# A hybrid decoder layer on one core: first loads in halves, key norms first, and a float32 block as three float32r products with the subtract on GpSimd

## The chip, the core and the metric

The kernel is one launch on one core of a Trainium2 chip. The metric is the device time of the launch in microseconds, from the first to the last instruction and what lies around it. Engines are named as in the profile: PE (TensorE matmuls), PEld (its weight loads), DVE (VectorE), ACT (ScalarE), POOL (GpSimd), SP (SyncE, which issues most transfers).

## What is computed

One layer over 256 tokens of width 2048, all in float32:

```python
h = _rmsnorm(x, ln1_g)
q, k, v, u = split(h @ w_in)             # 1024 | 256 | 256 | 1024 columns
q = _rmsnorm(q per head, q_norm_g); k = _rmsnorm(k per head, k_norm_g)
y_attn = _sliding_window_attention(q, k, v, attn_sinks, rel_bias)   # window 128
y_ssm = _s5_mixer(u, ...)                # 64 groups of 16 channels, 64 complex states, GELU, GLU
mixed = concat(_rmsnorm(y_attn, attn_out_g), _rmsnorm(y_ssm, ssm_out_g))
x = x + mixed @ w_out
h2 = _rmsnorm(x, ln2_g)
out = x + (silu(h2 @ w_ff_gate) * (h2 @ w_ff_up)) @ w_ff_down
```

Only the first part matters here: the projection to u (two blocks of 512 columns, `w_u`), the S5 mixer that feeds on u, the projection to q, k and v (three blocks of 512, `w_qkv`), and the norms of keys and queries.

## The kernel before

**Products.** A projection goes in blocks of 512 output columns. For both token tiles (t = 0, 1; 128 tokens each) a block sums 16 products of 128 rows of the weights. Weights come in pieces of two such row groups (`KD = 2`, 512 KB, tile `w`, four buffers), loaded by SP in the order of use (`Weights.fetch`, L436).

Most blocks run through `block` (L497): each factor is split in a high part that float32r holds exactly and a low part, and three float32r products stand for the float32 one: high x high (L513), high x low weight (L514), low x high weight (L515). `Weights._piece` splits a piece: ACT casts the high part (`whi`, L462), DVE subtracts it from the piece (`wlo`, L463). Both have two buffers (`split`), so that a cast waits until PE is done with the piece two before. A piece is 2 row groups x 2 token tiles x 3 = 12 products.

The two blocks of u run through `block32` (L522) instead: plain float32 products of `xt` (x transposed, scaled by the norm's weights) and the unsplit pieces, L530. The trace shows two passes for each such product. `xt` is four tiles that share memory with `sm` and `qn`, hence their names in the rows. `hT` and `lT` are the high and low part of `xt` (`split_x`, L605 and L606), which the w_qkv blocks use.

**S5.** The scan over 256 tokens is turned into small matrices: `tables` makes powers of the state's factor from a chain of small DVE and ACT steps; `matrices(q, h)` makes, for a quarter q of the channel groups and a half h of it, `cm` (L242, L243) and `bm` (L249, L250) on DVE from those tables and the coefficients, 128x1024 elements a step; PE multiplies and transposes them (`pk` L254, `pt_bm` L264). `tokens(q)` fetches u again from DRAM (`ut`, issued on POOL's queue, L283), where ACT's queue has put it (`ud`, L645); `states` and `outputs` do the scan and its outputs (`px`, `pa`, `pb`, `zz`, `hh`, `py`). The products of tokens within a chunk need a matrix `mt` that POOL's queue moves by way of DRAM (`kd` L272, `mt` L276).

**Order.** The program is written with priorities (`prio`) and a scheduler sets a fixed order for every engine. What POOL's or DVE's next instruction waits for holds up all behind it. The S5 steps (`STEPS`, priority 20,000) are spread among the matmuls of the u blocks (30,000 and 32,000) and the w_qkv blocks (60,000). The coefficients of quarters 2 and 3 are loaded into the memory of `xt` once that is free.

**Norms of keys and queries** (L703 to L728, priority 65,000). For each token tile: squares of its keys (ACT, L713), sums per head (DVE, L715), mean and epsilon (L716), the power -0.5 on POOL (L717, 128x4); the same for the queries (128x16); a scaling of the queries' factors (L718); the keys' scaling (L721). Then the keys are transposed on PE (`pt_k`, L725).

**Start.** SP issues the constants (`pack`, L391), then by turns a quarter of `xT` and a piece of `w_u`; ACT squares the quarter, DVE scales it in place (L601).

Of the kernel before, what the change touches and what calls it, by code (L numbers as in the profile page):

```python
# [10 lines left out]
F32 = mybir.dt.float32  # L11
F32R = mybir.dt.float32r
AF = mybir.ActivationFunctionType
ALU = mybir.AluOpType
AX = mybir.AxisListType
# [3 lines left out]
P = 128  # L19
D = 2048  # L20
L = 256
NT = L // P
HD = 64
NH = 16
NKV = 4
# [9 lines left out]
EPS = 1e-6  # L35
NEG = -1e30
NB = 512
KD = 2
# [21 lines left out]
def dap(t, dims, off=0):  # L60
    return bass.AP(t.tensor, t.offset + off, [list(d) for d in dims])


def bc(ap, pos, n):
    dims = [list(d) for d in ap.ap]
    dims.insert(pos, [0, n])
    return bass.AP(ap.tensor, ap.offset, dims)
# [319 lines left out]
def consts(tc, nc, cp, ins):  # L387

    c = {}
    pack = cp.tile([P, sum(n for _, n in COLS)], F32, name="pack")  # L390
    nc.sync.dma_start(pack, ins["c_pack"])  # L391
    at = 0
    for name, n in COLS:
        c[name] = pack[:, at : at + n]
        at += n
    c["halfpi"] = cp.tile([P, 1], F32, name="halfpi")
    nc.vector.memset(c["halfpi"], math.pi / 2)
    c["mhalf"] = cp.tile([P, NH + NKV], F32, name="mhalf")
    nc.vector.memset(c["mhalf"], -0.5)
    c["ones"] = cp.tile([P, 32], F32, name="ones")  # L400
    nc.vector.memset(c["ones"], 1.0)
    c["v32"] = cp.tile([P, 2], F32, name="v32")
    nc.vector.memset(c["v32"], 1.0 / 32)
    return c
# [20 lines left out]
class Weights:  # L425
# [5 lines left out]
        self.place = -100_000  # L431
        self.marks = []

    def fetch(self, src):
        w = self.raw.tile([P, KD, NB], F32, name="w", tag="w")
        self.nc.sync.dma_start(w, src)  # L436
        self.ready.append(w)

    def whole(self, src):
# [6 lines left out]
        self.marks.append([None])  # L446
        return [w[:, i] for i in range(KD)]

    def piece(self, src):
        was, self.tc.cur_priority = self.tc.cur_priority, self.place  # L450
        out = self._piece(src)
        self.place, self.tc.cur_priority = self.tc.cur_priority, was
        return out

    def _piece(self, src):
        nc = self.nc
        if not self.ready:
            self.fetch(src)
        w = self.ready.pop(0)
        hi = self.split.tile([P, KD, NB], F32R, name="whi", tag="whi")  # L460
        lo = self.split.tile([P, KD, NB], F32R, name="wlo", tag="wlo")
        self.marks.append([nc.scalar.copy(hi, w).ins])  # L462
        nc.vector.tensor_tensor(lo, w, hi.bitcast(F32), op=ALU.subtract)  # L463
        return [(hi[:, i], lo[:, i]) for i in range(KD)]


# [1 line left out]
def layer_kernel(ctx: ExitStack, tc: tile.TileContext, ins, out):  # L468
    nc = tc.nc
    v, s, pe = nc.vector, nc.scalar, nc.tensor  # L470
# [7 lines left out]
    wts = Weights(tc, nc, raw, split)  # L478

    @contextmanager  # L480
    def prio(at):

        was, tc.cur_priority = tc.cur_priority, at
        try:
            yield
        finally:
            tc.cur_priority = was
# [6 lines left out]
        nc.gpsimd.tensor_tensor(r, t, cst["mhalf"][:, :cols], op=ALU.pow)  # L494
        return r

    def block(hi, lo, wsrc, k0=0, behind=None, apart=False):  # L497


        acc = [ps.tile([P, NB], F32, name=f"acc{t}", tag="mm") for t in range(NT)]  # L500
        nk = KD * len(wsrc)
        k = 0
        for n, src in enumerate(wsrc):
            parts = wts.piece(src)
            turns = [(i, t) for i in range(KD) for t in range(NT)]
            if apart and n == len(wsrc) - 1:
                turns.sort(key=lambda it: it[1])
            for i, t in turns:
                whi, wlo = parts[i]
                xh = hi[:, k0 + k + i, t * P : (t + 1) * P]  # L510
                xl = lo[:, k0 + k + i, t * P : (t + 1) * P]
                first, last = k + i == 0, k + i == nk - 1
                mm = pe.matmul(acc[t], lhsT=xh, rhs=whi, start=first, stop=False)  # L513
                pe.matmul(acc[t], lhsT=xh, rhs=wlo, start=False, stop=False)  # L514
                pe.matmul(acc[t], lhsT=xl, rhs=whi, start=False, stop=last)  # L515
            k += KD
            wts.marks[-1].append(mm.ins)
            if behind and n in behind:
                behind[n](mm.ins)
        return acc  # L520

    def block32(x, wsrc):  # L522

        acc = [ps.tile([P, NB], F32, name=f"acc{t}", tag="mm") for t in range(NT)]
        nk = KD * len(wsrc)
        k = 0
        for src in wsrc:
            for w in wts.whole(src):
                for t in range(NT):
                    mm = pe.matmul(acc[t], lhsT=x(k)[:, t * P : (t + 1) * P], rhs=w, start=k == 0, stop=k == nk - 1)  # L530
                k += 1
            wts.marks[-1].append(mm.ins)
        return acc

    def pieces(w, nb, kg0, kgs):
        return [w[nb, kg] for kg in range(kg0, kg0 + kgs)]
# [33 lines left out]
    qn = [rt.tile([P, AW], F32, name=f"qn{t}") for t in range(NT)]  # L570
    kvn = [rt.tile([P, 2 * NKV * HD], F32, name=f"kvn{t}") for t in range(NT)]
# [4 lines left out]
    hT = stat.tile([P, D // P, L], F32R, name="hT", tag="shi")  # L576
    lT = stat.tile([P, D // P, L], F32R, name="lT", tag="slo")
    xt = [(sm + qn)[i].rearrange("p (k l) -> p k l", l=L) for i in range(4)]
    with prio(-300_000):
        cst = consts(tc, nc, cpool, ins)  # L580
        ident, g1 = cst["ident"], cst["g1"]
        ssm = Ssm(tc, nc, sp, ps, dpool, ins, cst)
        first = pieces(ins["w_u"], 0, 0, 4)
        for k4 in range(4):
            nc.sync.dma_start(xt[k4], ins["xT"][:, 4 * k4 : 4 * k4 + 4])
            wts.fetch(first[k4])
            if k4 == 0:
                ssm.load()
        ssm.coefficients(0, nc.sync)
    with prio(-99_990):  # L590
# [12 lines left out]
    def split_x(k4):  # L603
        ks = slice(4 * k4, 4 * k4 + 4)
        s.copy(hT[:, ks], xt[k4])  # L605
        v.tensor_tensor(lT[:, ks], xt[k4], hT[:, ks].bitcast(F32), op=ALU.subtract)  # L606
# [28 lines left out]
        nc.gpsimd.dma_start(td, mk)  # L635


    ngc = G // GC
    for nb in range(SW // NB):
        with prio(30_000 + 2_000 * nb):  # L640
            acc = block32(lambda k: xt[k // 4][:, k % 4], pieces(ins["w_u"], nb, 0, 16 // KD))
            for t in range(NT):
                un = kvn[t] if nb else sp.tile([P, NB], F32, name="un", tag="hh", bufs=2)
                s.activation(un, acc[t], AF.Copy, scale=r1[:, t : t + 1])
                nc.scalar.dma_start(ssm.ud[nb * (NB // UB) : (nb + 1) * (NB // UB), t * P : (t + 1) * P]  # L645
                                    .rearrange("b p x -> p b x"), un.rearrange("p (b x) -> p b x", x=UB))
    with prio(20_100):
        for k4 in range(4):
            split_x(k4)
        for q in range(2, ngc):  # L650
            ssm.coefficients(q, nc.sync, sm[q - 2])
    with prio(60_000):
# [47 lines left out]


    kT = at.tile([P, NKV // 2, 2, L], F32, name="kT")
    rq = []  # L703
    with prio(65_000):
        nc.gpsimd.memset(kT, 0.0)
        sk = at.tile([P, NH], F32, name="sk")
        nc.gpsimd.dma_start(sk, dap(ins["attn_sinks"], [[0, P], [1, NH]]))
        for t in range(NT):
            sh = at.tile([P, NH + NKV], F32, name=f"sh{t}")
            r_ = at.tile([P, NH + NKV], F32, name=f"rqk{t}")  # L710
            for src, o, n in ((kvn[t][:, : NKV * HD], NH, NKV), (qn[t], 0, NH)):
                sq = at.tile([P, n * HD], F32, name="sq", tag="lg", bufs=2)
                s.activation(sq, src, AF.Square)  # L713
                part = sh[:, o : o + n]
                v.tensor_reduce(part, sq.rearrange("p (h d) -> p h d", d=HD), axis=AX.X, op=ALU.add)  # L715
                v.tensor_scalar(part, part, 1.0 / HD, EPS, op0=ALU.mult, op1=ALU.add)  # L716
                nc.gpsimd.tensor_tensor(r_[:, o : o + n], part, cst["mhalf"][:, :n], op=ALU.pow)  # L717
            v.tensor_scalar_mul(r_[:, :NH], r_[:, :NH], HD**-0.5)  # L718
            rq.append(r_)
            kk = kvn[t][:, : NKV * HD].rearrange("p (h d) -> p h d", d=HD)  # L720
            v.tensor_tensor(kk, kk, bc(r_[:, NH:], 2, HD), op=ALU.mult)  # L721
        pt = ps.tile([P, 2, L], F32, name="pt_k", **WORK)
        for i in range(2):
            for t in range(NT):
                pe.transpose(pt[:, i, t * P : (t + 1) * P], kvn[t][:, i * P : (i + 1) * P], ident)  # L725
        for a in range(2):
            ks = slice(a * HD, (a + 1) * HD)
            s.activation(kT[ks, :, a], pt[ks], AF.Copy, scale=cst["qkg"][ks, 1:2])  # L728
# [67 lines left out]
    with prio(70_000):  # L796
        lg = [weights(0)]
# [166 lines left out]
```

## Time and profile before

| | us |
|---|---|
| median of 3 runs | 1066.72 (1064.7 to 1066.95) |
| the profiled execution | 1064.85 |
| its span, first to last instruction | 1063.1 |
| PE busy | 1043.2 (98%) |
| PEld busy | 820.8 (77%) |
| DVE busy | 610.9 (57%) |
| ACT busy | 485.4 (46%) |
| POOL busy | 56.1 (5%) |

The granted clock of PE is 0.999 of full speed over the span. A busy PE is not PE at its peak: products overlap in the pipeline, and their ends are modelled. What one costs is read from start to start. Shares over the whole span mix stages: the two u blocks and the w_qkv blocks lie in the first 175 us, the long feed-forward stage behind them is another matter.

### The profile page before, as it was taken

The page shows a single profiled execution, that of the slowest core. Times are in us where ns is not written, and L with a number is a line of the kernel's source. Part 1 is how long each engine was busy: PE and PEld are TensorE (multiplying, and loading weights), DVE is VectorE, ACT ScalarE, POOL GpSimd, SP SyncE. Part 2 cuts the span into 40 slices and gives each one's busy share as a digit, 9 for nine tenths or more (in the row PEclk, how much of TensorE's full clock was granted, in tenths as well). Part 3 has the DMA queues.
Part 4 walks back from the last instruction along what each step waited for, and adds up shares of the span by engine and source line. Part 5 has one row for each costly group of instructions (what it writes and reads, how often), then busy time and mean ns, then how long its engine had stood idle before and what let it go on. Part 6 is the DMA issues. An engine that isn't in the chain of part 4 may idle for free.

```text
span 1063.1 us, 13209 instructions
## 1 busy us (share of the span) xinstructions
PE 1043.2 (98%) x5048; PEld 820.8 (77%) x5048; DVE 610.9 (57%) x755; ACT 485.4 (46%) x665; POOL 56.1 (5%) x87
## 2 busy tenths in 40 slices
PE   7999988999999999999999999999999999999998
PEld 3457776767788888888888888888888888888886
DVE  6988975788556454445554455545555444444443
ACT  5244556665445444444444444444444333333332
POOL 2030325000000000000000000000000000000000
PEclk9999999999999999999999999999999999999999
DMA  7677567434455556555555555555655556565653
GB/s 268 191 197 237 152 180 267 165 109 139 158 189 167 182 193 189 189 183 194 189 189 195 180 197 185 193 191 184 198 181 196 179 190 207 195 201 195 203 192 101
DMA packets 62015, 199.08 MB, mean 187 GB/s; under 512 B 11328, under 2 KB 14000, under 8 KB 61632
## 3 DMA queue, kind: packets, MB, share of 16 engines
q1 hardware_dynamic: 52800, 184.89, 53.3%
q0 software_dynamic: 3264, 9.29, 3.3%
q10 hardware_dynamic: 5888, 4.06, 1.3%
q8 instruction: 39, 0.64, 0.3%
q14 instruction: 24, 0.20, 0.1%
HBM read 193.47 MB, written 4.74 MB: 186 GB/s over the span
## 4 chain that ended last, share of the span: by engine, by line
PE 85%; DVE 8%; ACT 2%; DMA 2%; issue 2%; POOL 1%; SPq 0%; DVEq 0%; POOLq 0%; ACTq 0%
PE acc L514 26%; PE acc L515 26%; PE acc L513 26%; PE acc L530 2%; DVE wlo L463 1%; PE pt_f L872 1%; DMA zd<-za 1%; POOL rqk L717 1%; PE po L786 1%; DVE bm L249 1%; ACT whi L462 1%; DVE cm L242 1%; DVE bm L250 1%; DVE tm L249 1%; DVE cm L243 1%
## 5 line engine op out<-in xcount | busy, mean ns | idle before, releaser
L463 DVE TENSOR_TENSOR wlo<-w,whi 128x1024 fp32r<-128x1024 f32 x328 | 401.7, 1225 | 407.4 <-ACT whi L462 407.1
L462 ACT CAST whi<-w 128x1024 fp32r<-128x1024 f32 x328 | 345.1, 1052 | 473.1 <-PE acc L515 461.4
L513 PE MATMUL acc<-whi,pTh 128*128 128x512 f32 x704 | 275.0, 391 | 0.0
L514 PE MATMUL acc<-wlo,pTh 128*128 128x512 f32 x704 | 274.0, 389 | 0.2 <-DVE wlo L463 0.2
L515 PE MATMUL acc<-whi,pTl 128*128 128x512 f32 x704 | 274.1, 390 | 0.1
L515 PEld LDWEIGHTS acc<-whi,pTl 128*128 128x128 f32 x704 | 132.1, 188 | 28.0 <-DVE pTl L564 0.5
L514 PEld LDWEIGHTS acc<-wlo,pTh 128*128 128x128 f32 x704 | 132.2, 188 | 27.6 <-DVE wlo L463 0.7
L513 PEld LDWEIGHTS acc<-whi,pTh 128*128 128x128 f32 x704 | 132.2, 188 | 27.6 <-ACT pTh L563 0.5
L513 PE MATMUL acc<-whi,fhi 128*128 128x512 f32 x352 | 139.0, 395 | 0.0
L514 PE MATMUL acc<-wlo,fhi 128*128 128x512 f32 x352 | 138.9, 395 | 0.0
L515 PE MATMUL acc<-whi,flo 128*128 128x512 f32 x352 | 138.9, 394 | 0.0
L515 PEld LDWEIGHTS acc<-whi,flo 128*128 128x128 f32 x352 | 66.3, 188 | 15.5
L513 PEld LDWEIGHTS acc<-whi,fhi 128*128 128x128 f32 x352 | 66.3, 188 | 15.5
L514 PEld LDWEIGHTS acc<-wlo,fhi 128*128 128x128 f32 x352 | 66.3, 188 | 15.3
L513 PE MATMUL acc<-whi,mT 128*128 128x512 f32 x128 | 50.9, 397 | 0.8 <-ACT mT L563 0.8
L514 PE MATMUL acc<-wlo,mT 128*128 128x512 f32 x128 | 50.5, 394 | 0.0
L515 PE MATMUL acc<-whi,nT 128*128 128x512 f32 x128 | 50.3, 394 | 0.0
L514 PE MATMUL acc<-wlo,hT 128*128 128x512 f32 x96 | 38.6, 402 | 2.8 <-DVE wlo L463 2.8
L515 PE MATMUL acc<-whi,lT 128*128 128x512 f32 x96 | 38.0, 396 | 0.0
L513 PE MATMUL acc<-whi,hT 128*128 128x512 f32 x96 | 37.7, 398 | 0.0
L530 PE MATMUL acc<-w,sm 128*128 128x512 f32 x64 | 30.7, 628 | 6.7 <-DVE sm L601 6.7
L884 ACT ACTIVATE sl<-acc,r 128x256 f32<-128x256 f32 x44 | 20.8, 472 | 20.7 <-PE acc L515 20.7
(258 smaller groups left out, 822.0 us busy)
## 6 DMA issues: line engine op xcount, KB each, us to landing
w<-in_w_gu SPq DMA_DIRECT2D x176, 512.0 KB, 3.3
w<-in_w_down SPq DMA_DIRECT2D x88, 512.0 KB, 3.4
w<-in_w_out SPq DMA_DIRECT2D x32, 512.0 KB, 3.3
w<-in_w_qkv SPq DMA_DIRECT2D x24, 512.0 KB, 4.3
w<-in_w_u SPq DMA_DIRECT2D x16, 512.0 KB, 4.0
w<-in_w_glu SPq DMA_DIRECT2D x8, 512.0 KB, 4.3
bias<-td POOLq DMA_DIRECT2D x4, 512.0 KB, 5.1
x<-in_x POOLq DMA_DIRECT2D x2, 1024.0 KB, 10.4
```

Source lines behind the costliest of these rows:

```text
L242: v.tensor_tensor(dst, bc(c[:, i, hs], 2, T), bc(e, 3, GP), op=ALU.mult)
L243: v.tensor_tensor(cmh[:, :, 1:], cmh[:, :, 1:], tm, op=ALU.subtract)
L249: v.tensor_tensor(dst, bc(b[:, i, hs], 2, T), bc(e, 3, GP), op=ALU.mult)
L250: v.tensor_tensor(bm2, bm2, tm2, op=ALU.add)
L462: self.marks.append([nc.scalar.copy(hi, w).ins])
L463: nc.vector.tensor_tensor(lo, w, hi.bitcast(F32), op=ALU.subtract)
L513: mm = pe.matmul(acc[t], lhsT=xh, rhs=whi, start=first, stop=False)
L514: pe.matmul(acc[t], lhsT=xh, rhs=wlo, start=False, stop=False)
L515: pe.matmul(acc[t], lhsT=xl, rhs=whi, start=False, stop=last)
L530: mm = pe.matmul(acc[t], lhsT=x(k)[:, t * P : (t + 1) * P], rhs=w, start=k == 0, stop=k == nk - 1)
L717: nc.gpsimd.tensor_tensor(r_[:, o : o + n], part, cst["mhalf"][:, :n], op=ALU.pow)
L884: s.activation(sl, acc[t][:, :256], AF.Silu, scale=r2[:, t : t + 1])
```

## The change

- The constants are loaded on ACT's queue. The first quarter of `xT` and the first piece of `w_u` come in halves, the first half of `xT` first. The small S5 inputs (`ssm.load`) are issued after the second quarter and piece.
- The second block of u runs through `block` with `hT` and `lT`: three float32r products, eight pieces cast on ACT, and their low parts subtracted on POOL (`rest=nc.gpsimd`). The split of `xt` is written ahead of the u blocks.
- The norms: keys of both token tiles first, with their scaling, then the queries of both.

```diff
-    nc.sync.dma_start(pack, ins["c_pack"])
+    nc.scalar.dma_start(pack, ins["c_pack"])
...
-    def fetch(self, src):
+    def fetch(self, src, parts=1):
         w = self.raw.tile([P, KD, NB], F32, name="w", tag="w")
-        self.nc.sync.dma_start(w, src)
+        n = KD // parts
+        for i in range(0, KD, n):
+            self.nc.sync.dma_start(w[:, i : i + n], src[:, i : i + n])
...
-        nc.vector.tensor_tensor(lo, w, hi.bitcast(F32), op=ALU.subtract)
+        rest.tensor_tensor(lo, w, hi.bitcast(F32), op=ALU.subtract)
...
         for k4 in range(4):
-            nc.sync.dma_start(xt[k4], ins["xT"][:, 4 * k4 : 4 * k4 + 4])
-            wts.fetch(first[k4])
             if k4 == 0:
+                nc.sync.dma_start(xt[0][:, :2], ins["xT"][:, :2])
+                wts.fetch(first[0], KD)
+                nc.sync.dma_start(xt[0][:, 2:], ins["xT"][:, 2:4])
+            else:
+                nc.sync.dma_start(xt[k4], ins["xT"][:, 4 * k4 : 4 * k4 + 4])
+            if k4:
+                wts.fetch(first[k4])
+            if k4 == 1:
                 ssm.load()
...
+    with prio(20_100):
+        for k4 in range(4):
+            split_x(k4)
     ngc = G // GC
     for nb in range(SW // NB):
         with prio(30_000 + 2_000 * nb):
-            acc = block32(lambda k: xt[k // 4][:, k % 4], pieces(ins["w_u"], nb, 0, 16 // KD))
+            src = pieces(ins["w_u"], nb, 0, 16 // KD)
+            if nb == 0:
+                acc = block32(lambda k: xt[k // 4][:, k % 4], src)
+            else:
+                acc = block(hT, lT, src, rest=nc.gpsimd)
...
+        def head_norms(t, src, o, n):
+            sq = at.tile([P, n * HD], F32, name="sq", tag="lg", bufs=2)
+            s.activation(sq, src, AF.Square)
+            part = sh[t][:, o : o + n]
+            v.tensor_reduce(part, sq.rearrange("p (h d) -> p h d", d=HD), axis=AX.X, op=ALU.add)
+            v.tensor_scalar(part, part, 1.0 / HD, EPS, op0=ALU.mult, op1=ALU.add)
+            nc.gpsimd.tensor_tensor(rq[t][:, o : o + n], part, cst["mhalf"][:, :n], op=ALU.pow)
+
+        for t in range(NT):
+            head_norms(t, kvn[t][:, : NKV * HD], NH, NKV)
+        for t in range(NT):
             kk = kvn[t][:, : NKV * HD].rearrange("p (h d) -> p h d", d=HD)
-            v.tensor_tensor(kk, kk, bc(r_[:, NH:], 2, HD), op=ALU.mult)
+            v.tensor_tensor(kk, kk, bc(rq[t][:, NH:], 2, HD), op=ALU.mult)
+        for t in range(NT):
+            head_norms(t, qn[t], 0, NH)
+            v.tensor_scalar_mul(rq[t][:, :NH], rq[t][:, :NH], HD**-0.5)
```

How the order moves at three places. POOL, behind the mask for the bias (`td`), before: transfers of u (`ut`) and of the S5 matrix (`kd`, `mt`):

```order
L494 TENSOR_TENSOR r_275<-r_a,mhalf 128x2
L635 DMA td<-mk 16x384
L283 DMA ut<-ud 128x512 x2
L272 DMA kd_107<-kt_105 128x1x64 x4
L276 DMA mt_111<-kd_107 16x256
```

and in the change, the low parts of the second u block (L465) among them:

```order
L643 DMA td<-mk 16x384
L465 TENSOR_TENSOR wlo<-w,whi 128x1024 x2
L283 DMA ut<-ud 128x512
L465 TENSOR_TENSOR wlo<-w,whi 128x1024 x2
L283 DMA ut<-ud 128x512
L465 TENSOR_TENSOR wlo<-w,whi 128x1024
L272 DMA kd_112<-kt_110 128x1x64 x3
L465 TENSOR_TENSOR wlo<-w,whi 128x1024
L272 DMA kd_112<-kt_110 128x1x64
L465 TENSOR_TENSOR wlo<-w,whi 128x1024
```

From the third on the subtracts stand behind transfers that have waits of their own; the eighth follows behind four of the `mt` transfers.

PE, from the end of the first u block (`acc_289`) into the second, before, where `pk` is the first half group's product of S5 matrices:

```order
L530 MATMUL acc_289<-w,qn_76 128x512
L530 MATMUL acc_336<-w,sm_79 128x512
L254 MATMUL pk<-cm,bm_853 32x128 x8
L264 MATMUL pt_bm<-pack,bm_853 128x128 x8
L530 MATMUL acc_337<-w,sm_79 128x512
```

and in the change, where eleven float32r products of the second block stand ahead of that group (the last two here):

```order
L515 MATMUL acc_347<-whi,hT 128x512
L516 MATMUL acc_347<-wlo,hT 128x512
L254 MATMUL pk<-cm,bm_951 32x128 x8
L264 MATMUL pt_bm<-pack,bm_951 128x128 x8
L517 MATMUL acc_347<-whi,lT 128x512
```

The groups of S5 keep their order on PE; the number of products between them changes. From the seventh half group on they stand at the same or nearly the same product of the w_qkv blocks as before.

ACT at the S5 tables, before (`qs` belongs to the sum of squares of x, `cm` to the first matrices, L162 is the last sine):

```order
L159 ACTIVATE wa<-wa 128x64
L547 COPY qs<-pq 128x256
L238 ACTIVATE cm<-sc,sign 128x8x16 x2
L605 CAST hT<-qn_76 128x1024
L160 ACT_TABLE_LOAD
L160 ACTIVATE wa<-wa 128x64
L161 ACTIVATE wa<-wa 128x64
L162 ACTIVATE wa<-wa,halfpi 128x64
```

and in the change:

```order
L613 CAST hT<-qn_76 128x1024
L549 COPY qs<-pq 128x256
L238 ACTIVATE cm<-sc,sign 128x8x16
L160 ACT_TABLE_LOAD
L160 ACTIVATE wa<-wa 128x64
L161 ACTIVATE wa<-wa 128x64
L238 ACTIVATE cm<-sc,sign 128x8x16
L162 ACTIVATE wa<-wa,halfpi 128x64
```

The copy and the two `cm` steps, which stood ahead of the last cast, now stand behind it.

## Rows read from the trace of the kernel before

**Rows 1.** busy time by windows: us, PE, PEld, DVE, ACT, POOL (instructions), PEclk, DMA share, GB/s

```profile
20.00:124.00 104.00, 103.13 (x630) 63.73 (x628) 95.73 (x145) 45.42 (x76) 23.11 (x44) 1.00 0.70 199
...
330.00:1063.10 733.10, 728.67 (x3231) 599.33 (x3229) 358.17 (x339) 305.26 (x329) 0.69 (x1) 1.00 0.58 188
```

**Rows 2.** waits of PE, 0 to 320 us: in total, times, longest

```profile
PE acc L514 <- DVE wlo L463: 3.5, 5, 2.2
```

**Rows 3.** timeline at the seventh half group: start us, us, engine, line, instruction [idle before it]

```profile
122.37 1.23 DVE L250 TENSOR_TENSOR bm<-bm,tm 128x1024 f32<-128x1024 f32 x1
...
124.11 0.64 PE L254 MATMUL pk<-cm,bm 128*32 128x128 f32 x16
```

**Rows 4.** timeline of PE: passes of float32 products, then float32r products

```profile
65.22 10.03 PE L530 MATMUL acc<-w,qn 128*128 128x512 f32 x23
...
146.17 0.39 PE L514 MATMUL acc<-wlo,hT 128*128 128x512 f32 x1
...
148.89 0.39 PE L514 MATMUL acc<-wlo,hT 128*128 128x512 f32 x1
```

**Rows 5.** groups by line: count | busy us, mean ns | idle before

```profile
L462 ACT CAST whi<-w 128x1024 fp32r<-128x1024 f32 x328 | 345.1, 1052 | 473.1 <-PE acc L515 461.4
...
L243 DVE TENSOR_TENSOR cm<-cm,tm 128x1024 f32<-128x1024 f32 x7 | 8.5, 1218 | 0.0
...
L705 POOL MEMSET kT<- 128x1024 f32 x1 | 1.0, 972 | 0.0
```

**Rows 6.** timeline of DVE and POOL, 178 to 187 us

```profile
178.52 3.92 POOL L717 TENSOR_TENSOR rqk<-sh,mhalf 128x16 f32<-128x16 f32 x2 [3.49 <-DVE sh L716]
...
178.63 1.23 DVE L463 TENSOR_TENSOR wlo<-w,whi 128x1024 fp32r<-128x1024 f32 x1
...
181.48 0.17 DVE L718 TENSOR_SCALAR rqk<-rqk 128x16 f32<-128x16 f32 x1 [0.50 <-POOL rqk L717]
...
182.89 1.22 DVE L463 TENSOR_TENSOR wlo<-w,whi 128x1024 fp32r<-128x1024 f32 x1
...
183.06 3.81 POOL L717 TENSOR_TENSOR rqk<-sh,mhalf 128x16 f32<-128x16 f32 x1 [0.62 <-DVE sh L716]
```

**Rows 7.** timeline of ACT and DVE at the S5 tables

```profile
17.43 0.37 ACT L547 COPY qs<-pq 128x256 f32<-128x256 f32 x1 [0.61 <-PE pq L544]
...
17.70 0.69 ACT L238 ACTIVATE cm<-sc,sign 128x128 f32<-128x128 f32 x2
...
20.45 0.54 DVE L633 TENSOR_TENSOR mk<-pb,mk 16x384 f32<-16x384 f32 x1
...
21.45 0.23 DVE L165 SCALAR_TENSOR_TENSOR wa<-wa 128x64 f32<-128x64 f32 x1
```

**Rows 8.** timeline of the first loads

```profile
0.75 0.39 SPq L391 DMA_DIRECT2D pack<-in_c_pack  x1
...
2.96 0.43 DVE L207 TENSOR_TENSOR dg<-pack 128x256 f32<-128x256 f32 x1 [1.65 <-DMA pack<-in_c_pack]
...
5.33 1.34 ACT L612 ACTIVATE sq<-sm 128x256 f32<-128x256 f32 x4 [3.09 <-DMA sm<-in_xT]
...
5.78 1.27 DVE L601 TENSOR_SCALAR sm<-sm,pack 128x256 f32<-128x256 f32 x4 [2.40 <-ACT sq L612]
...
6.75 8.09 PE L530 MATMUL acc<-w,sm 128*128 128x512 f32 x14 [6.75 <-DVE sm L601]
```

**Rows 9.** timeline of PE and DVE at the key and query norms

```profile
182.95 0.55 PE L725 MATMUL pt_k<-pack,kvn 128*128 128x128 f32 x3 [1.37 <-DVE kvn L721]
...
186.90 0.17 DVE L718 TENSOR_SCALAR rqk<-rqk 128x16 f32<-128x16 f32 x1 [2.79 <-POOL rqk L717]
```

**Rows 10.** waits of DVE, 20 to 124 us: in total, times, longest

```profile
DVE wlo L463 <- ACT whi L462: 5.1, 4, 1.7
```

**Rows 11.** timeline of ACT's and POOL's queues at u

```profile
42.85 0.37 ACTq L645 DMA_DIRECT2D ud<-un  x1
...
46.60 0.57 POOL L283 DMA_DIRECT2D ut<-ud  x1 [24.77 <-DMA ud<-un]
```

More of the change, by code (lines that the diff above doesn't have):

```diff
@@ L447, in whole, with piece, _piece @@
         return [w[:, i] for i in range(KD)]
-    def piece(self, src):
+    def piece(self, src, rest=None):
         was, self.tc.cur_priority = self.tc.cur_priority, self.place
-        out = self._piece(src)
+        out = self._piece(src, rest or self.nc.vector)
         self.place, self.tc.cur_priority = self.tc.cur_priority, was
         return out
-    def _piece(self, src):
+    def _piece(self, src, rest):
         nc = self.nc
@@ L495, in rsqrt_mean, with block @@
         return r
-    def block(hi, lo, wsrc, k0=0, behind=None, apart=False):
+    def block(hi, lo, wsrc, k0=0, behind=None, apart=False, rest=None):
         acc = [ps.tile([P, NB], F32, name=f"acc{t}", tag="mm") for t in range(NT)]
@@ L503, in block @@
         for n, src in enumerate(wsrc):
-            parts = wts.piece(src)
+            parts = wts.piece(src, rest)
             turns = [(i, t) for i in range(KD) for t in range(NT)]
@@ L647, in layer_kernel @@
     with prio(20_100):
-        for k4 in range(4):
-            split_x(k4)
         for q in range(2, ngc):
@@ L702, in layer_kernel @@
     kT = at.tile([P, NKV // 2, 2, L], F32, name="kT")
-    rq = []
     with prio(65_000):
@@ L707, in layer_kernel @@
         nc.gpsimd.dma_start(sk, dap(ins["attn_sinks"], [[0, P], [1, NH]]))
-        for t in range(NT):
[L709 to L719, printed above, removed]
+        sh = [at.tile([P, NH + NKV], F32, name=f"sh{t}") for t in range(NT)]
+        rq = [at.tile([P, NH + NKV], F32, name=f"rqk{t}") for t in range(NT)]
+        def head_norms(t, src, o, n):
[5 more added lines that the diff above has]
+            nc.gpsimd.tensor_tensor(rq[t][:, o : o + n], part, cst["mhalf"][:, :n], op=ALU.pow)
+        for t in range(NT):
+            head_norms(t, kvn[t][:, : NKV * HD], NH, NKV)
+        for t in range(NT):
             kk = kvn[t][:, : NKV * HD].rearrange("p (h d) -> p h d", d=HD)
-            v.tensor_tensor(kk, kk, bc(r_[:, NH:], 2, HD), op=ALU.mult)
+            v.tensor_tensor(kk, kk, bc(rq[t][:, NH:], 2, HD), op=ALU.mult)
+        for t in range(NT):
+            head_norms(t, qn[t], 0, NH)
+            v.tensor_scalar_mul(rq[t][:, :NH], rq[t][:, :NH], HD**-0.5)
         pt = ps.tile([P, 2, L], F32, name="pt_k", **WORK)
```

## The prediction

> **What bounds the kernel now.** I read the table of windows first. In the last 733.1 us PE is busy for 728.7 [rows 1]: nothing there is touched, so whatever PE gains or loses before 330 us is the change in the time. In the stretch from 20 to 124 us two engines are full at once: PE 103.13 of 104.00 us, DVE 95.73, which leaves DVE 8.3 us of idle time. POOL has 23.1 us of work there [rows 1]. So the question is not only how much PE work goes, but whether DVE can follow.
>
> Next the waits of PE up to 320 us: the largest behind the start is 3.5 us in all, for low parts of weights [rows 2]. So PE sets the pace, with few holes. How close DVE is behind shows at the seventh half group of S5 matrices: its last DVE step (L250) starts at 122.37 and takes 1.23, its first matmul on PE runs at 124.11 [rows 3]. That place, half a microsecond after DVE, is my yardstick: when does PE pass it in the change? In both orders the same DVE instructions and 150 products of the w_qkv blocks stand ahead of it.
>
> **The change part by part.** *Second column block of u.* It ran as 32 float32 products of two passes each; 23 passes take 10.03 us, so a pass 0.43 [rows 4] and the block 64 x 0.43 = 27.5 us. It becomes 96 float32r products; from 146.17 to 148.89 there are twelve, 0.227 each [rows 4], so 21.8 us. PE saves 5.7 us. It needs eight more casts of 1.05 us on ACT [rows 5] and eight subtracts. ACT is 45 us busy of 104 in the stretch [rows 1], and a piece on PE lasts 12 x 0.227 = 2.7 us, so the casts cost nothing while they follow each other in time; without that cover each is 1.05.
>
> *The subtract on GpSimd.* No subtract of 128x1024 runs on POOL in this trace. From below: POOL writes 128x1024 in 0.97 us [rows 5], one stream. From above: two reads and one write one after the other at that rate, 2.9. On DVE the same operation takes 1.23 [rows 6]. I take two streams, 1.94 us, since a read and a write can overlap but the two reads are the extra: 15.5 us for eight. POOL has the time. The question is what it does to DVE, whose steps in this stretch are nearly all tensor_tensors with two operands in SBUF (L243 is one of four such lines, 1.22 us each [rows 5]), as the subtract is.
>
> For that the trace has one telling pair. The power of 128x16 on POOL begins at 178.52 and has released DVE at 181.48, 2.9 us; the next one, the same shape, begins at 183.06 and takes 3.81 [rows 6]. The difference of 0.9 us fits the subtract that DVE had begun at 182.89, which ran 1.05 us into it [rows 6]. POOL seems to have stood until DVE was done. In the other direction DVE began a subtract 0.11 us after POOL began its power and took 1.23 as always [rows 6]; but the power reads only 16 elements per partition, at its start, so that says little of an operation that reads 1024.
>
> The Trainium skill, SBUF — State Buffer, "Who interferes with whom", says that a DVE instruction with two SBUF inputs and a GpSimd instruction that reads SBUF exclude each other, and that whichever comes second is blocked for the whole of the first. The longer power agrees with it; the DVE subtract at 178.63, unhindered for the 2.9 us of the first power, does not, so the "whole instruction" is not what this trace shows. GPSIMD Engine Reference, "Elementwise — side-by-side cycle accounting", gives 4497 ns for a float32 tensor_tensor of 2048 elements; an estimate from that figure is 2.25 us per subtract, and the sum below would be 1075.9 instead of 1073.4. No run here shows it.
>
> So I take it that subtract and DVE step go one after the other, whichever comes first. Then DVE's and POOL's work adds up: at the yardstick DVE needs 124.1 - 8.3 (all its idle time used) + 15.5 + 1.3 = 132.6 us. The 1.3 is a later start of the S5 tables: in the new ACT order the copy qs and one cm row stand between the last cast and the table load, and another cm row ahead of the last sine (L162), three steps of some 0.27 from start to start, 0.8 us, and DVE waits for that sine with L165; and the 0.54 us of L633, which lay in DVE's wait, now stands behind the tables [rows 7].
>
> *First loads.* Transfers are issued from 0.75; the constants (122 KB) land 2.2 us after their issue, the first 512 KB of x at 5.33, and PE begins at 6.75 [rows 8]. With the constants on ACT's queue, the first half of x goes out at 0.75 and needs 256 KB less: from 2.2 us for 122 KB and 4.6 us for 634 KB I work out 3.4 us for 378 KB, landing about 4.2; one square (a quarter of 1.34) and one scaling (a quarter of 1.27) later, and with half a weight tile another 1.2 us behind, PE begins near 5.3: 1.4 us sooner (ends: 0, if the weights land as late as now, and 1.5). On DVE it gives nothing: the second half of x and the cast behind it end as late as now.
>
> PE by itself would therefore be at the yardstick at 124.1 - 5.7 - 1.4 = 117.0. DVE at 132.6 comes later and sets it: 8.5 us later than now.
>
> *Key norms first.* PE's wait of 1.37 us for the keys goes [rows 9], since both small powers and scalings now run before the queries' squares. But the two powers of 128x16 now follow each other, DVE's two scalings of them (L718 waited 2.79 us for the second [rows 9]) stand side by side ahead of eight score rows (L756), and the next low part is behind all of them; now it stood behind one. PE can lose 2 to 3 us there. I take the sum as zero, with ends of -2.4 and +3.
>
> Sum, against the profiled execution's own 1064.85 us (its median of three runs is 1066.72, 1.9 more): 1064.85 + 8.5 + 0 = 1073.4. About 0.2%, 2.1 us, is what a measurement of this kernel can tell from no change.
>
> **The rivals.** *Free port, faster.* POOL and DVE do not hold each other up: the low parts cost DVE nothing. For it speaks the subtract at 178.63 that ran at its usual length beside a power [rows 6]; against it the power that took 0.9 us longer. DVE is then at the yardstick at 124.1 - 8.3 + 1.3 = 117.1, PE at 117.0. DVE's waits don't all go: 5.1 us of them are for casts that wait for PE [rows 10], and I leave 1.5. The time is 1064.85 - 7.0 + 1.5 = 1059.3. It decides itself by the cost per subtract on DVE: above 0.9 us each (7.1 / 8) nothing is left of the gain.
>
> *POOL's queue is the new wait.* Port free, but subtracts stand in order behind transfers. The third is behind ut, which waits until both ud writes have landed: now ut begins at 46.60, 3.4 us after the second write's issue ends [rows 11]. The write moves ahead of the copies of bm, some 1.5 us earlier, so ut ends near 45.7 and the subtract near 47.6; PE, which begins the block near 38.7, wants it at 38.7 + 24 x 0.227 + 1.6 for the first group = 45.8. That is 1.8 us; the fifth to eighth, behind the second ut, kd and mt, some 0.5 us each. About 4 us go: 1063.3, no change.
>
> *Half a price.* The port is held for one stream only, 0.97 us a subtract: DVE at 117.1 + 7.8 = 124.9, 0.8 later than now: 1065.6, no change.
>
> **How the numbers follow.** One after the other (1073.4): 0.53; the longer power is the only row that bears on two operations of this kind that meet, and it speaks for it. Free port (1059.3): 0.27. Queue (1063.3): 0.12. Half a price (1065.6): 0.08. The likeliest case alone runs from 1068 (0.6 us less per subtract and 8.3 us of idle time used) to 1081 (2.9 us per subtract). Cases of both signs hold most of the chance, so the range reaches from 1058, just under the free port, to 1081. Faster by over 0.2% is the free port and a quarter of the queue, 0.30; within 0.2% the rest of the queue and most of half a price, 0.16; slower 0.54.
>
> **What would show it.** If I am right, DVE's tensor_tensors of 128x1024 between 33 and 75 us are longer than 1.22 or begin late while a subtract is on POOL, or POOL's subtracts are far longer than 2 us when DVE is busy; PE waits several microseconds for bm (L250) or for wlo of the second block; the seventh group's first matmul is at about 132. If the subtracts take about 2 us, DVE's steps stay at 1.22 with no holes, and the seventh group is before 119, the port was free and I am wrong. Right or wrong apart from that: 0.227 per product in the second block, PE's first product near 5.3, and a wait of PE in the first block of w_glu for the low part behind the score rows.

## The result and the profile after

The changed kernel takes 1083.5 us (median of four runs, 1080.81 to 1085.05), the kernel before 1066.84 on the same chip: 1.0154 times as long, 95% interval 1.0136 to 1.0172. The span of the profiled run is 1081.2 us against 1063.1, 18.1 us more. The direction was forecast, the size was not: the forecast was +8.5 us on the profiled run, and the median lies 2.5 us above the top of the range.

The table of windows, read as before [rows 1] (us; PE, PEld, DVE, ACT, POOL busy; granted clock of PE; DMA share; GB/s):

```profile
20.00:124.00 104.00, 85.45 (x517) 59.67 (x516) 90.07 (x130) 43.04 (x70) 45.71 (x39) 0.92 0.56 165
330.00:1081.20 751.20, 746.33 (x3322) 613.61 (x3321) 371.53 (x361) 317.16 (x353) 0.70 (x1) 1.00 0.58 187
```

PE was full from 20 to 124 us; now it is idle for 18.5 of 104, and DVE isn't full either. What comes late there is pushed behind 330 us, where PE is still full. The waits of PE from 20 to 142 us (in total, times, longest) say for what:

```profile
PE acc L516 <- POOL wlo L465: 9.5, 3, 7.3
PE pk L254 <- DVE bm L250: 6.9, 2, 5.1
PE acc L516 <- DVE wlo L465: 2.5, 3, 1.5
```

Two of the three are signs that the prediction named: low parts of the second u block, and `bm`. The row of the eight GpSimd subtracts (duration in ns: shortest, median, longest; first and last start):

```profile
L465 POOL TENSOR_TENSOR wlo<-w,whi x8: 2354/2798/10236, 36.8 to 86.6; 128x1024 fp32r<-128x1024 f32 x8
```

By itself one takes 2.35 us; the first took 10.2. The timeline of DVE (start, duration) shows what it met. The first subtract began at 36.83 and ended at 47.06, the third began at 55.46:

```profile
35.90 1.21 DVE L249 TENSOR_TENSOR bm<-sb,ft 128x1024 f32<-128x1024 f32 x1
37.04 1.21 DVE L243 TENSOR_TENSOR cm<-cm,tm 128x1024 f32<-128x1024 f32 x1
...
43.31 1.21 DVE L242 TENSOR_TENSOR tm<-sc,lam 128x1024 f32<-128x1024 f32 x1
44.45 0.41 DVE L222 TENSOR_SCALAR kr<-an 128x512 f32<-128x512 f32 x1
53.23 0.19 DVE L260 TENSOR_TENSOR kt<-kt,dg 128x32 f32<-128x32 f32 x1 [8.37 <-ACT kt L259]
...
55.08 1.22 DVE L249 TENSOR_TENSOR tm<-sb,ft 128x1024 f32<-128x1024 f32 x1
56.22 3.40 DVE L242 TENSOR_TENSOR cm<-sc,lam 128x1024 f32<-128x1024 f32 x1
59.54 3.40 DVE L250 TENSOR_TENSOR bm<-bm,tm 128x1024 f32<-128x1024 f32 x1
62.87 3.38 DVE L249 TENSOR_TENSOR bm<-sb,ft 128x1024 f32<-128x1024 f32 x1
...
88.24 0.79 DVE L260 TENSOR_TENSOR kt<-kt,dg 128x32 f32<-128x32 f32 x1 [1.09 <-ACT kt L259]
```

From 37 to 44.9 DVE's steps run one behind the other at their usual lengths (1.21 us for 128x1024), and the subtract stands. At 44.86 DVE has nothing ready, and 2.2 us later the subtract is done. From 56 on it is DVE that stands: 3.40 is 1.22 and 2.2 us of somebody else's subtract. Five DVE steps are so, 10.9 us in all; with a small one at 88.24 (0.79 instead of 0.18) it is 11.5.

The timeline of PE behind the first subtract, and the windows around it:

```profile
47.70 0.63 PE L517 MATMUL acc<-whi,lT 128*128 128x512 f32 x1
48.13 0.63 PE L515 MATMUL acc<-whi,hT 128*128 128x512 f32 x1
...
54.07 0.39 PE L515 MATMUL acc<-whi,hT 128*128 128x512 f32 x1
54.30 0.40 PE L516 MATMUL acc<-wlo,hT 128*128 128x512 f32 x1
```

```profile
40.00:47.00 7.00, 0.00 (x0) 0.00 (x0) 4.86 (x6) 0.65 (x1) 7.00 (x1) 0.71 0.38 75
47.00:53.00 6.00, 5.89 (x28) 4.04 (x29) 0.00 (x0) 0.17 (x1) 2.91 (x3) 0.50 0.83 278
53.00:76.00 23.00, 16.71 (x93) 12.77 (x91) 22.77 (x14) 11.86 (x18) 17.19 (x10) 1.00 0.43 139
76.00:84.00 8.00, 5.22 (x60) 4.43 (x60) 7.38 (x8) 2.13 (x4) 1.96 (x4) 0.57 0.30 86
```

PE is idle for 7 us, its granted clock goes from 1.00 to 0.50 (2.4 to 1.2 GHz), and the next products step 0.43 us apart instead of 0.23. After the 5.1 us wait for `bm`, at 76 to 84, the same again (0.57). With 5.9 us of busy PE at half clock, and some 5 more there, I estimate that about 5 us of PE's time go to the clock. No run takes the clock apart from the waits ahead of it, so what these 5 us are worth at the end is not shown.

The yardstick, the seventh half group of S5 matrices, starts at 142.0 (row of `pk`, 141 to 143 us), 17.9 us later than before [rows 3]: the whole loss lies ahead of it.

```profile
L254 PE MATMUL pk<-cm,bm x16: 272/273/297, 142.0 to 142.3; 128*32 128x128 f32 x16
```

### The profile page after: what moved, and what is told of

It is laid out like the page before. It is cut to its first block, busy times and chain, and to the rows that moved or that the text cites. A ratio compares the mean times of both kernels' runs of the same rounds, so it can differ in the third digit from the quotient of the medians.

```text
span 1081.2 us, 13301 instructions
## 1 busy us (share of the span) xinstructions
PE 1042.5 (96%) x5080; PEld 829.7 (77%) x5080; DVE 621.9 (58%) x755; ACT 494.0 (46%) x673; POOL 84.7 (8%) x95
## 4 chain that ended last, share of the span: by engine, by line
PE 83%; DVE 7%; issue 5%; DMA 2%; POOL 1%; ACT 1%; SPq 0%; DVEq 0%; ACTq 0%; POOLq 0%
PE acc L516 26%; PE acc L517 26%; PE acc L515 25%; DVE wlo L465 2%; PE acc L532 1%; DMA w<-in_w_u 1%; POOL wlo L465 1%; PE pt_f L889 1%; PE po L803 1%; DVE cm L243 1%; DVE bm L250 1%; DVE bm L249 1%; DVE tm L249 1%; ACT whi L464 0%; PE pp L797 0%
## 5 line engine op out<-in xcount | busy, mean ns | idle before, releaser
L465 DVE TENSOR_TENSOR wlo<-w,whi 128x1024 fp32r<-128x1024 f32 x328 | 401.7, 1225 | 409.9 <-ACT whi L464 409.6
L464 ACT CAST whi<-w 128x1024 fp32r<-128x1024 f32 x336 | 353.6, 1052 | 475.2 <-PE acc L517 458.1
L515 PEld LDWEIGHTS acc<-whi,fhi 128*128 128x128 f32 x352 | 66.3, 188 | 15.5
L516 PE MATMUL acc<-wlo,hT 128*128 128x512 f32 x128 | 52.7, 411 | 14.4 <-POOL wlo L465 9.5
L517 PE MATMUL acc<-whi,lT 128*128 128x512 f32 x128 | 51.4, 401 | 0.0
L515 PE MATMUL acc<-whi,hT 128*128 128x512 f32 x128 | 51.1, 405 | 0.0
L516 PEld LDWEIGHTS acc<-wlo,hT 128*128 128x128 f32 x128 | 24.6, 192 | 23.4 <-POOL wlo L465 10.9
L465 POOL TENSOR_TENSOR wlo<-w,whi 128x1024 fp32r<-128x1024 f32 x8 | 29.6, 3705 | 16.4 <-ACT whi L464 16.3
```

Of the source, the lines that this page charges most:

```text
L465: rest.tensor_tensor(lo, w, hi.bitcast(F32), op=ALU.subtract)
```

## Experiments

Theory A: a GpSimd subtract and a DVE step shut each other out, and this is the whole loss. Rivals: float32r products in this place are the trouble, whoever makes the low parts (B); the 10.2 us are a first use of the instruction (C); DVE isn't slowed, only PE's waits for low parts cost (D). Later the question was whether the long first stand is a cost of its own.

### Low parts on DVE again

```diff
-                acc = block(hT, lT, src, rest=nc.gpsimd)
+                acc = block(hT, lT, src)
```

> The change with one thing undone: the low parts of the second u block are subtracted on DVE again. Theory A (a GpSimd subtract and a DVE tensor_tensor with two SBUF operands shut each other out, and PE then stands for low parts that come late): the eight 3.4 us wlo waits and DVE steps are gone; DVE has 8 x 1.22 = 9.8 us more of its own work instead of 8 x 2.35 = 18.8 us of blocked time, no DVE 128x1024 step is longer than 1.25 us, the seventh half group is at 124.1 - 8.3 + 9.8 + 1.3 = 127, time about 1068 (1065 to 1071). Theory B (float32r products in this place are themselves the trouble, because PE in its order waits for every low part, whoever makes it): PE still waits over 8 us for wlo in the second u block and the time stays above 1078.

Measured: 1067.63 us, 1.0018 times before (1.0009 to 1.0028). No DVE step is longer than 1.23 us. From 20 to 124 us PE is busy again and DVE fuller than ever:

```profile
20.00:124.00 104.00, 99.83 (x671) 70.55 (x669) 101.28 (x155) 54.40 (x87) 19.21 (x37) 1.00 0.63 194
```

The time is as theory A had it, and B falls. That the subtracts are on GpSimd costs 1.0154 - 1.0018 of 1066, about 14.5 us; all the rest of the change costs 2. The seventh half group comes at 131.3, not at 127; but 38 more products of the w_qkv blocks stand ahead of it than before (8.6 us at 0.227), so its place can't be set beside 124.1.

### A subtract at the start

```diff
+        early = cpool.tile([P, 8], F32, name="early")
+        early_r = cpool.tile([P, 8], F32R, name="early_r")
+        nc.gpsimd.memset(early, 1.0)
+        nc.gpsimd.tensor_tensor(early_r, early, early, op=ALU.subtract)
```

> The change with a subtract of 128x8 on GpSimd added at the very start, so that GpSimd has done a subtract with a float32r result before the first real one. Theory A (the first real subtract stood 10.2 us because DVE ran nine steps without a gap): nothing moves, the first one takes 9 to 11 us again, PE waits 7 us for it, time 1082 to 1085. Theory C (the 10.2 us are a first use, 7.9 us on top of 2.35): the first takes 2.4 to 3.5 us, PE waits for it at most 1.5 us, its clock stays up, the time falls by 8 to 12 us, to about 1073.

Measured: 1.0177 (1.0162 to 1.0192). The first real subtract comes at 34.77, 2 us earlier, and lasts until 47.04, 12.3 us (theory A had said 9 to 11): DVE's row of steps ends at 44.84, and 2.2 us later the subtract is done, whenever it began. C falls.

### Spare subtracts and spare copies in the kernel before

In `whole`, for the second u block, with the result unused (the copies: `tensor_copy(lo, w)`):

```diff
+        if spare:
+            lo = self.split.tile([P, KD, NB], F32R, name="wlo", tag="wlo")
+            self.nc.gpsimd.tensor_tensor(lo, w, w, op=ALU.subtract)
```

> The kernel before, with eight GpSimd subtracts of 128x1024 added that nobody reads: each piece of the second u block minus itself. PE keeps its float32 products and waits for none of them. Theory A: the port alone costs: DVE steps of 128x1024 that meet a subtract take 3.4 us instead of 1.22, each such meeting 2.2 us; with the 8.3 us of idle time DVE had, 3 to 10 us late at the seventh half group, time 1068 to 1076, DVE busy above 100 us from 20 to 124. A subtract that finds DVE busy without a gap may stand 5 us or more. Theory D (DVE is not slowed, what costs in the change is only that PE waits for low parts): DVE steps stay at 1.22 and the time stays within 1064 to 1068.

> As the spare subtracts, but each a copy on GpSimd of 128x1024 with one operand. If only the instruction's reads of SBUF matter, theory A expects the copies to block DVE like the subtracts, each for its own length (1 to 2.4 us), time 1067 to 1076. If it takes two operands on both sides to shut each other out, DVE steps stay at 1.22 and the time is that of before, 1065 to 1068.

Measured: 1.0294 (1.0279 to 1.031) and 1.0252 (1.0235 to 1.0269), far worse than any theory gave, although PE waits for none of them. Rows of the subtracts, then of the copies:

```profile
L447 POOL TENSOR_TENSOR wlo<-w x8: 1887/2202/25638, 33.8 to 84.9; 128x1024 fp32r<-128x1024 f32 x8
```

```profile
L447 POOL CAST wlo<-w x8: 1035/1215/24839, 34.0 to 81.7; 128x1024 fp32r<-128x1024 f32 x8
```

The first one stands for 25.6 (24.8) us; in the run with subtracts 25 DVE steps begin and end behind it. PE isn't stalled by it, DVE doesn't run dry, and so it stands longer than in the change. Behind it and three more subtracts on POOL's queue is the transfer of `ut`, issued at 66.92 instead of 46.60 [rows 11], and PE's wait, in the run with subtracts, is this:

```profile
PE pu L291 <- ACT uq L289: 26.1, 2, 18.9
```

So this is mostly the price of a stuck queue, the rival that I had priced at 4 us. How it ended, on DVE (subtracts, then copies):

```profile
56.49 1.22 DVE L250 TENSOR_TENSOR bm<-bm,tm 128x1024 f32<-128x1024 f32 x1
57.74 2.80 DVE L242 TENSOR_TENSOR tm<-sc,lam 128x1024 f32<-128x1024 f32 x1
60.58 2.80 DVE L243 TENSOR_TENSOR cm<-cm,tm 128x1024 f32<-128x1024 f32 x1
```

```profile
58.01 1.94 DVE L242 TENSOR_TENSOR tm<-sc,lam 128x1024 f32<-128x1024 f32 x1
```

The steps ahead overlapped by 0.08 us (one starts 1.135 after the other and takes 1.22); the one at 57.74 starts 0.03 us after the end of the last. There GpSimd got in. A subtract of a piece from itself takes 1.89 us alone and holds DVE for 1.6, a copy 1.04 and 0.7: one operand is enough. D falls, as DVE is slowed; but that PE's waits don't matter isn't shown, they are the larger part here.

### The first two low parts on DVE, six on GpSimd

```diff
-            parts = wts.piece(src, rest)
+            parts = wts.piece(src, rest if n > 1 else None)
```

> The change, with the first two low parts of the second u block on DVE and the other six on GpSimd. Theory A in its stronger form (a GpSimd subtract that comes while DVE runs its steps without a gap stands until DVE has one): without PE's first stall DVE does not run dry, so one of the next subtracts stands instead, 5 us or more, with PE behind it; time 1073 to 1085. Theory A in the plain form (each subtract and each DVE step that meet go one after the other, and the 10.2 us were chance): no subtract longer than 3.6 us, six meetings of 2.2 us against 8.3 us of idle time, time 1069 to 1073.

Measured: 1.0191 (1.0177 to 1.0206). Timeline of POOL:

```profile
43.32 6.12 POOL L465 TENSOR_TENSOR wlo<-w,whi 128x1024 fp32r<-128x1024 f32 x1 [9.07 <-ACT whi L464]
...
49.99 9.45 POOL L465 TENSOR_TENSOR wlo<-w,whi 128x1024 fp32r<-128x1024 f32 x1
...
59.97 2.39 POOL L465 TENSOR_TENSOR wlo<-w,whi 128x1024 fp32r<-128x1024 f32 x1
```

The stronger form holds, though the time, 1086.34, is 1.3 us above its range: the stand moves to whichever subtract meets a row of DVE steps.

### Subtracts in quarters

```diff
-        rest.tensor_tensor(lo, w, hi.bitcast(F32), op=ALU.subtract)
...
+            for i in range(KD):
+                for h in range(0, NB, NB // 2):
+                    at = slice(h, h + NB // 2)
+                    rest.tensor_tensor(lo[:, i, at], w[:, i, at], hi[:, i, at].bitcast(F32), op=ALU.subtract)
```

> The change, with each of the eight GpSimd subtracts cut into four of 128x256. If GpSimd stands because DVE does not let go between its steps, the first quarter stands as long as the whole did (to 44.9 us, DVE's first gap), and PE waits about 7 us there again; behind it DVE steps that meet a quarter are longer by 0.6 us instead of 2.2, but meet more of them; time 1078 to 1088. If a long instruction is itself what cannot get in, quarters get in between DVE's steps at once, none stands over 2 us, and the time is 1070 to 1075.

Measured: 1.0168 (1.0152 to 1.0185).

```profile
L471 POOL TENSOR_TENSOR wlo<-w,whi x32: 714/766/8974, 36.7 to 87.1; 128x256 fp32r<-128x256 f32 x32
```

The first quarter stands for 9.0 us, to the same end of DVE's row; the others take 0.72 alone, and DVE steps that meet one take 1.75, 0.53 more. Shorter instructions don't help here: four quarters cost DVE 2.1 us, as much as a whole subtract.

### DVE made to give way

```diff
+        if rest is not nc.vector:
+            nc.vector.tensor_copy(self.seen, lo[:, 0, :1].bitcast(F32))
...
+    wts.seen = cpool.tile([P, 1], F32, name="seen")
```

> The change, with one copy of a single column on DVE behind each GpSimd subtract, which reads its result: DVE stops there until the subtract is done, so no subtract can be kept waiting by a row of DVE steps. If the long first stand and what hangs on it (PE idle for 7.3 us, its clock down behind it) are a cost of their own: no subtract above 3.6 us, PE waits at most 1.5 us for the first, seventh half group at 124.1 - 8.3 + 18.8 (8 x 2.35) + 1.3 + 1 (DVE waiting for casts) = 137, time 1076 to 1079. If DVE's and POOL's work one after the other is the whole loss: the time stays at 1081 to 1085.

Measured: 1.0174 (1.016 to 1.0188); 1084.4 us. My theory by now, that the first stand is a cost of its own, fell. No subtract stands longer than 3.5 us, and the seventh half group comes at 139.8 instead of 142.0, but the end is no sooner. Waits of PE from 20 to 142 us (in the change 6.9 for `bm`, 9.5 for low parts from POOL):

```profile
PE pk L254 <- DVE bm L250: 10.4, 2, 5.3
...
PE acc L519 <- POOL wlo L465: 2.9, 1, 2.9
```

Giving way has a price of its own, DVE's waits for the subtracts:

```profile
DVE seen L467 <- POOL wlo L465: 6.8, 3, 2.3
```

Of 6.6 us saved at PE's waits for low parts 3.5 go to `bm`, and 2.2 still show at the half group (142.0 - 139.8), where my theory had expected 5. At the first score product (`pl`) 1.2 are left, at the last 0.2; what takes them there I didn't follow. So this way of taking the stand off brings nothing; that no way could is not shown.

### GpSimd where DVE is half idle

The kernel before, with the fifth low part of the eight in each of the 22 w_gu blocks on GpSimd.

```diff
-            parts = wts.piece(src)
+            parts = wts.piece(src, rest if n == 4 else None)
...
-        acc = block(pT, qTl, pieces(ins["w_gu"], nb, 0, 16 // KD), behind={2: turn} if len(held) == 2 else None)
+        acc = block(pT, qTl, pieces(ins["w_gu"], nb, 0, 16 // KD), rest=nc.gpsimd, behind={2: turn} if len(held) == 2 else None)
```

> The kernel before with one low part of eight in each of the 22 w_gu blocks on GpSimd: a stretch in which DVE is busy half of the time and has gaps before every low part. Theory A: GpSimd gets the port at once, each subtract takes 2.35 to 2.4 us (up to 3.5 where a DVE step of 0.48 to 1.22 us goes first), DVE's other steps are 1.22 or wait once; the low part is ready 1.1 us later than now, of which about 0.5 us are spare, so PE waits 0.6 to 0.9 us for each: 13 to 20 us, ratio 1.012 to 1.019. If a subtract stands far longer here too (over 5 us), DVE need not be gapless for that.

Measured: 1.0125 (1.0112 to 1.0138), 13.3 us, 0.6 for each subtract.

```profile
L463 POOL TENSOR_TENSOR wlo<-w,whi x22: 2379/2382/2415, 336.3 to 814.8; 128x1024 fp32r<-128x1024 f32 x22
```

```profile
PE acc L514 <- POOL wlo L463: 8.5, 12, 0.7
```

None met a DVE step with two operands in SBUF; 2.38 is the price alone. In ten of the 22, two DVE steps ran beside the subtract, which take one operand from SBUF and one from PSUM (`flo<-pt_f,fhi`, L876), and neither side was longer: 0.69 and 0.68 us, 0.68 in the kernel before. Even so each subtract cost time. I estimate why: a cast of 1.05 and a subtract of 2.38 make 3.4 us, and a piece lasts 12 x 0.227 = 2.7 on PE, all that two buffers leave. PE's waits for these low parts, 8.5 us, are the larger part of the 13.3; the rest I didn't trace.

### The other two parts alone, and with float32

`u2_f32` has the change's loads and norms and keeps the second u block in float32; `loads_only` and `norms_only` are the kernel before with one of the two, edited as in the change's diff. `u2_f32` against the change:

```diff
-            if nb == 0:
-                acc = block32(lambda k: xt[k // 4][:, k % 4], src)
-            else:
-                acc = block(hT, lT, src, rest=nc.gpsimd)
+            acc = block32(lambda k: xt[k // 4][:, k % 4], src)
```

> The change without its middle part: the second u block in float32 products as before, the new first loads and the new norms. By the terms of the prediction: PE begins at 5.4 instead of 6.75, all of it kept at the seventh half group (122.7 instead of 124.1) if DVE's 8.3 us of idle time cover its later S5 tables; norms 0 (-2.4 to +3). Time 1063.5 under the profiled run's own terms, ratio 0.9987 (0.997 to 1.002). If the loads and norms cost part of the 16 us that the change lost, the ratio is above 1.004.

> The kernel before with the new first loads alone. If what PE gains at its start is kept: PE's first product at 5.4, seventh half group 1.4 us sooner, ratio 0.9987. If DVE, whose work starts no sooner, sets that place as well: no change, ratio 0.9995 to 1.001.

> The kernel before with the key norms first alone. The wait of 1.4 us before the key transposes (pt_k) goes. If the two query powers of 128x16 back to back on GpSimd then hold up DVE's low part for w_glu, PE waits 2 to 3 us for it instead: ratio 1.000 to 1.002. If not: ratio 0.998 to 0.999.

Measured: together 1.0025 (1.0013 to 1.0037); loads alone 0.9994 (0.9985 to 1.0002), norms alone 0.9988 (0.9978 to 0.9999). With the loads alone PE begins at 5.41, but its seventh half group comes at 126.0, not 122.7: what PE gained at the start was not kept there. Two more products of w_qkv stand ahead of it (0.5 us), and the profiled run was 1.3 us above its median. The two parts don't add up: together (with the split of `xt` written ahead, as in the change) they are 4.6 us slower than the sum of both. `u2_f32` has its first score product (`pl`, 184.1 us) 3.6 us before the loads alone, and the last product of the attention's output (`po`, 267.0 us) 5.2 after it. So the loss lies among score rows and w_glu low parts, whose order differs in each; I didn't follow it further.

### The block alone with DVE, whole and half

The kernel before with the second u block in float32r and low parts on DVE; the same with key norms first; then with only the last four pieces of the block in float32r, without and with the norms. The whole block, then the half (in a copy of the loop of `block` and `block32`, with `plain` = 4):

```diff
+            acc = block(hT, lT, src) if nb else block32(lambda k: xt[k // 4][:, k % 4], src)
```

```diff
+            parts = wts.whole(src) if n < plain else wts.piece(src)
```

> The kernel before with the second u block in float32r products, low parts on DVE, first loads and norms as before. PE saves 5.7 us there; DVE gets 8 x 1.22 = 9.8 us of work against 8.3 us of idle time, so DVE sets the seventh half group at 124.1 - 8.3 + 9.8 = 125.6 at best: 1.5 us late, ratio 1.0014 (0.999 to 1.004). If DVE's waits go beyond that, because PE no longer makes it wait, the ratio is below 0.998.

> The same with the key norms first. If the two parts add up: 1.5 us from the block, -1.3 us from the norms (measured alone at 0.9988), ratio 1.000. If the gain of the norms hangs on how the score rows meet the w_glu low parts, as the pair of loads and norms suggests (0.9994 and 0.9988 alone, 1.0025 together), it is anywhere from 0.997 to 1.004.

> The kernel before; of the second u block the first four pieces stay in float32, the last four are three float32r products with their low parts on DVE. PE saves 5.7 / 2 = 2.8 us, DVE gets 4 x 1.22 = 4.9 us, less than its 8.3 us of idle time. If DVE's idle time is usable: seventh half group 2 to 2.8 us sooner, ratio 0.9975 (0.997 to 0.9985). If the idle time lies where the steps that PE waits for cannot use it, as eight low parts on DVE suggest (1.0011): ratio 0.999 to 1.001.

> The same with the key norms first. If both add up, -1.3 us more than without: ratio 0.996 to 0.9985. If the norms' gain hangs on the order of the rows around the first w_glu block, as the earlier pairs suggest: no better than without, 0.999 to 1.002.

Measured: 1.0011 (1.0003 to 1.002), 1.0018 (1.0009 to 1.0026), 1.0037 (1.0026 to 1.0048), 1.0037 (1.0024 to 1.0049). The block by itself is no gain with DVE either, and half of it is worse than all, against my sum. The windows of `block_dve`, then of `half_dve`:

```profile
20.00:124.00 104.00, 100.90 (x670) 70.66 (x669) 100.69 (x149) 53.14 (x85) 21.96 (x43) 1.00 0.67 200
```

```profile
20.00:124.00 104.00, 102.12 (x649) 66.92 (x648) 97.55 (x153) 48.86 (x78) 23.02 (x44) 1.00 0.66 200
```

DVE's 8.3 us of idle time [rows 1] were filled in part: 3.3 are left with eight low parts, 6.5 with four. What is lost comes later. The seventh half group is at 128.6 with 26 more products of w_qkv ahead of it, and at 127.8 with 14 more; at 0.227 each that is 1.4 us sooner and 0.5 later than before. Behind it `half_dve` loses nearly 5 us: PE waits 2.8 us for `hh` and 3.8 for gelu's `sm` (161 and 181 us; before, 0.2 and 1.1 at most). Only the norms alone lie below the kernel before with their whole interval, by 1.3 us, and its end is 0.9999: a gain that can hardly be told from none. The loads alone, 0.6 us below, can't be told from it.

## Why the prediction was right in its direction and wrong in its size

- **Right: one after the other.** Subtract and DVE step exclude each other, as the one longer power [rows 6] suggested. The Trainium skill, SBUF — State Buffer, "Who interferes with whom", calls it an exclusive lock that is held for the whole instruction. The steps of 3.40 agree with that; that whoever starts first has it does not agree with the 10.2 and 25.6 us, in which eight and 25 DVE steps that began after the subtract ran ahead of it. My reading of the power at 178.52, that "the 'whole instruction' is not what this trace shows", was drawn from an instruction that reads 16 elements, and didn't hold for one that reads 1024.
- **Wrong by 1.6 us: the price.** I took 1.94 us a subtract, 15.5 for eight. Alone it takes 2.35, and a meeting costs DVE 2.2. DVE stood for 11.5 us in its steps and was idle for another 5.6 while a subtract ran, 17.1 in all. The Trainium skill, GPSIMD Engine Reference, "Elementwise — side-by-side cycle accounting", gives 4497 ns for twice the elements; the estimate from it, 2.25 us, was nearer to the 2.35 than my two streams at the rate of a memset.
- **Wrong by 8.4 us: the step that failed.** "all its idle time used". The windows up to the seventh half group, before and in the change, say that DVE was busy for 95.8 of 104.1 us and for 108.0 of 122.0:

```profile
20.00:124.10 104.10, 103.23 (x630) 63.73 (x628) 95.83 (x145) 45.42 (x76) 23.11 (x44) 1.00 0.70 200
```

```profile
20.00:142.00 122.00, 102.92 (x667) 72.80 (x667) 108.00 (x151) 54.95 (x88) 52.49 (x52) 0.93 0.57 167
```

  Of the 108.0, 11.5 are standing, so DVE's own work is 96.5, 0.7 more than before (1.3 forecast). Of the 14.0 us of idle time 5.6 lie beside a subtract; in the other 8.4 neither works. That is as much as DVE's whole idle time before: none of it was used. DVE's waits in that window:

```profile
DVE kt L260 <- ACT kt L259: 9.5, 2, 8.4
DVE wlo L465 <- ACT whi L464: 2.2, 1, 2.2
```

  The largest hole in which neither works is 49.4 to 53.2: DVE waits for `kt`, that is for PE, which had waited for the subtract, which had waited for DVE, and PE runs at half clock. In the forecast two engines shared one gate; in the run a third stands between them and hands each one's delay to the other. 132.6 + 1.6 + 8.4 - 0.6 = 142.0. DVE's idle time is not useless by itself: with the low parts on DVE it falls to 2.7 us (`low_on_dve`) and 3.3 (`block_dve`). With the low parts on GpSimd none of it was used. In `give_way`, where DVE waits for the subtracts instead, 4.9 us of it remain, and the half group is 2.2 us sooner.
- **Right: 5.7 us less on PE** for the block; its products step 0.23 us where the clock is full. Nothing came of it, as DVE set the place.
- **Right in size, not kept: the start.** PE begins at 5.40 (5.3 forecast). I took 1.4 us into PE's side of the sum only, and it was lost there.
- **Norms: zero** held in the change, in part by luck: 17.9 us late at the yardstick, 18.1 at the end. PE's wait for the keys [rows 9] is gone, and a wait of 3.0 us for a low part behind the score rows has come. By itself the part gave 1.3 us; `u2_f32` is 3.3 us behind the loads alone (its split of `xt` is moved too). The part has no price of its own that holds in every order; these two lie within or near the ends that I gave, -2.4 and +3.
- **The rivals.** The free port is refuted by the steps of 3.40. The queue alone is not the loss here, but it is where a stand does most harm, as the spare subtracts show. Half a price is refuted by 2.2 us per meeting.

## What to carry to other kernels

A GpSimd elementwise step is no free helper of a DVE that is busy with steps of two operands in SBUF: count it as DVE work, at 2.2 us here where DVE itself needed 1.22, and ask first what stands behind it on GpSimd's queue. Idle time of an engine is not a budget when it lies in waits for another that waits in turn; add up a cover only if you can name the hole and the step that would fall into it. Low parts on DVE found such holes, those on GpSimd made new ones. A place on PE, such as my half group, tells of time only where as many products stand ahead of it. Gains of parts that reorder the same rows are not to be added.

## Not expected of the hardware

- A GpSimd instruction can stand while a row of DVE steps that began after it runs: 10.2 us and eight steps in the change, 25.6 us and 25 steps with the spare subtracts; in other places the two took turns from the first boundary (at 56.2 in the change). It got in when DVE ran dry (44.9) or at a gap of 0.03 us (57.74, spare subtracts); but at 56.2 the steps overlap as elsewhere. It happens to DVE too: in `quarters` four GpSimd quarters, 0.76 us each, ran while one DVE step stood (4.61 instead of 1.22, the row below). What decides the turn stays open.

```profile
72.10 4.61 DVE L250 TENSOR_TENSOR bm<-bm,tm 128x1024 f32<-128x1024 f32 x1
```

- A GpSimd copy with one operand shuts out DVE's two-operand steps as well: 1.94 instead of 1.22. DVE steps with one operand in SBUF and one in PSUM ran beside subtracts at no cost to either (`gu_one_in_eight`).
- A 128x1024 subtract on GpSimd takes 2.35 us from two tiles, 1.89 from one tile twice, a copy 1.04.
